# Modulation accumulations queued behind the last split of weights, and each partition sum behind a named panel's gate, in the last phase of a two-layer backbone

## The chip, the cores and the metric

The kernel runs on one core of a Trainium2 chip. A core has TensorE (PE in the profile; its weight loads are the row PEld), VectorE (DVE), ScalarE (ACT), GpSimd (POOL) and SyncE (SP), each with its own queue that it works through in order, and 16 DMA engines. The metric is the device time of one execution in microseconds (us); the time of a kernel is the median of its runs.

## What is computed

Two layers act on 256 latent rows of 1024 columns, and the first also on 256 context rows. Each layer is feed-forward, mixer, feed-forward; the mixer is attention in layer 0 and a short gated convolution in layer 1. All data are float32.

```python
for i in range(2):
    m = (silu(c) @ ada_w[i] + ada_b[i]).reshape(9, D)     # shift, scale, gate of three sub-layers
    x = half_step_ffn(x, m[0], m[1], m[2], ...)
    hx = modulate(x, m[3], m[4])                          # x * (1 + scale) + shift
    y = attention(hx) if i == 0 else short_conv_mixer(hx)
    x = layer_norm(ALPHA * x + m[5] * y)
    x = half_step_ffn(x, m[6], m[7], m[8], ...)
# half_step_ffn: a, u = modulate(x) @ w_in; y = (silu(a) * u) @ w_out;
#                x = layer_norm(ALPHA * x + 0.5 * gate * y)
```

The nine vectors of a layer come from a product of one row with a 1024 x 9216 matrix. Here they are called the modulation, and vector m of layer l is (l, m).

## The kernel before

**Products.** Every float32 weight tile is split into a high part (ACT, line 216) and the rest, the low part (DVE, line 219), and a product is made of three matmuls: high by high, low by high, high by low (lines 170 to 173, `mmu`). A unit is 256 rows by 512 columns of a weight, 512 KB. It is loaded by SP (line 211), then split in two halves on each engine, 128x512 each. Raw tiles have 4 buffers, high parts 4 and low parts 5, and two more pairs in the last phase. The names are `w1r`, `w1h`, `w1l` for the first matrix of a feed-forward, `w2...` for the second, `wc...` and `wo...` for those of the convolution.

**Stages.** A first matrix is worked through in panels (`panels`): panel p is 512 columns, its units are used for both latent tiles t = 0 and 1, and at its end ACT and DVE make the gate, `sil` = silu(a) * u (lines 503 and 504), once for each tile. A feed-forward has eleven panels, p = 0 to 10. The second matrix is worked through by `out_gemm` in a skewed order in which tile 1 follows five units behind tile 0, so that a unit stays in use longer. At its end follow the residual and the norm (`res`, `x`, `st`, `mv` on DVE, `rs` on POOL, `x` again), the transposes `hT`, and `h`, `hTh`, `hTl`, the input of the next panels. PE's order is written out by hand; the order on the other engines is made by the framework's scheduler when the program is built.

**The last phase** holds the second feed-forward of layer 0 (panels from about 590 us, second matrix from 714), the first of layer 1 (from 778, second matrix from 900), the convolution (from 964) and the last feed-forward (from 1060).

**The modulation stream.** `ada` loads `ada_w` in slices of 128 rows by 1024 columns (`ar`, 512 KB, three buffers) and adds each, times its element of silu(c), to an accumulator `acc` on DVE (line 301 for a vector's first slice, line 303 for the others), two instructions of 128x512 for a slice. Eight slices make a vector. A step of the stream is taken at a rate for each unit of PE work; in the last phase the rate is `ADA_SLOWEST`. An accumulation may not stand ahead of the newest gate multiply on DVE (`gate_ins`). In the last phase, marked by `on_pool`, `sum_up` then makes the sum over the 128 partitions on POOL (line 349, `PARTITION_ALL_REDUCE` in the profile), adds it to the bias in DRAM (line 350) and closes with a small instruction (line 352). It is called when a feed-forward's panel p in `SUM_AT` is done, at the end of the panels (`need`), and in the convolution at the end of a panel from the second on. Five vectors are made so: (1, 4) to (1, 7) in one stream, and (1, 8) in the last feed-forward.

Of the kernel before, what the change touches and what calls it, by code (L numbers as in the profile page):

```python
# [10 lines left out]
F32 = mybir.dt.float32  # L11
# [3 lines left out]
ALU = mybir.AluOpType  # L15
# [3 lines left out]
P = 128  # L19
# [13 lines left out]
WB = (4, 5, 5)  # L33
PB = {"mm": 3, "at": 3, "tp": 2}
W_EARLY = 40
ADA_SLOW, ADA_FAST, ADA_SLOWEST = 3, 0.6, 0.115
KT_IDLE = 6
BIAS_AT = 24
ADA_LATE = 20
# [29 lines left out]
E0 = (0,)  # L69
E2 = (0, 5, 7)  # L70
HOLD = 4
SUM_AT = (2, 5, 8)


@with_exitstack
def backbone_kernel(
# [6 lines left out]
    nc = tc.nc  # L83
# [10 lines left out]

    uid = [0]
    w_early = [0]
    last_split = []
    ext = [1, 0]
    ada_late = [0]

# [84 lines left out]
    def wunit(srcs, kn, s, own=None, wd=512, put_off=False):  # L185

        raw = wp.tile([P, UN], F32, tag="wr", bufs=WB[0], name=nm(s + "r"))
        if own:  # L190
            hs, ls = ([act(F32R, s + c) for _ in range(kn)] for c in "hl")
            rv = raw[:, :kn * 512].rearrange("p (a b) -> p a b", a=kn)
            with tc.high_priority(offset=w_early[0]):
                for src, c in srcs:
                    sync.dma_start(rv[:, :, c:c + src.shape[2]], src)
                for i in range(kn):
                    with queued(own[i]):
                        nc.scalar.activation(hs[i], rv[:, i], AF.Copy)
                        nc.vector.tensor_tensor(out=ls[i], in0=rv[:, i], in1=hs[i].bitcast(F32), op=ALU.subtract)
            return Parts(hs), Parts(ls)  # L200
        ext[1] += 1
        if ext[0] and ext[1] % (5 + ext[0]) in (E0 if ext[0] == 1 else E2):
            hi = hp.tile([P, UN], F32R, tag="whx", bufs=ext[0], name=nm(s + "h"))
            lo = hp.tile([P, UN], F32R, tag="wlx", bufs=ext[0], name=nm(s + "l"))
        else:
            hi = wp.tile([P, UN], F32R, tag="wh", bufs=WB[1], name=nm(s + "h"))
            lo = wp.tile([P, UN], F32R, tag="wl", bufs=WB[2], name=nm(s + "l"))
        rv, hv, lv = (t[:, :kn * wd].rearrange("p (a b) -> p a b", a=kn) for t in (raw, hi, lo))
        with tc.high_priority(offset=w_early[0]):
            for src, c in srcs:  # L210
                sync.dma_start(rv[:, :, c:c + src.shape[2]], src)

        def parts():
            m = kn * wd
            for a in range(0, m, m // W_HI):
                last_split[:] = [nc.scalar.activation(hi[:, a:a + m // W_HI], raw[:, a:a + m // W_HI], AF.Copy)]  # L216
            for a in range(0, m, m // W_LO):
                b = a + m // W_LO
                nc.vector.tensor_tensor(out=lo[:, a:b], in0=raw[:, a:b], in1=hi[:, a:b].bitcast(F32), op=ALU.subtract)  # L219
            return hv, lv  # L220

        if put_off:
            return parts
        with tc.high_priority(offset=w_early[0]):
            return parts()
# [18 lines left out]
    lnc = cp.tile([P, 2], F32, tag="lnc", name="lnc")  # L244
# [4 lines left out]
    warm = cp.tile([1, 1], F32, tag="warm", name="warm")  # L249
# [27 lines left out]

    bias_rows = []
    on_pool = [False]
    sums = []  # L280
    gate_ins = []

    def ada(vecs):
# [3 lines left out]

        def accumulate(l, m, k, w):
            with ExitStack() as st:
                for i in gate_ins:  # L290
                    st.enter_context(tc.issue_after(i.ins))
                for i, vec in enumerate(vecs):
                    if vec[:2] != (l, m):
                        continue
                    if k == 0:
                        acc[i] = hp.tile([P, D], F32, tag="acc", bufs=2, name=nm("acc"))
                    sc = cst[:, k, vec[2]:vec[2] + 1]
                    for h in range(2):
                        src, a = (c[:, h * 512:(h + 1) * 512] for c in (w, acc[i]))
                        if k == 0:  # L300
                            nc.vector.tensor_scalar(a, src, sc, None, op0=ALU.mult)
                        else:
                            nc.vector.scalar_tensor_tensor(out=a, in0=src, scalar=sc, in1=a,  # L303
                                                           op0=ALU.mult, op1=ALU.add)
            if on_pool[0] and k == KC - 1:
                sums.extend((vec, acc[i]) for i, vec in enumerate(vecs) if vec[:2] == (l, m))
# [36 lines left out]
        yield 1  # L343

    def sum_up():
        while sums:
            (l, m, v), a = sums.pop(0)
            red = hp.tile([P, D], F32, tag="red", name=nm("red"))
            nc.gpsimd.partition_all_reduce(red, a, P, ReduceOp.add)
            nc.gpsimd.dma_start(scr[l][v:v + 1, m * D:(m + 1) * D], red[0:1], accum_op=ALU.add)  # L350
            if not sums:
                nc.gpsimd.tensor_tensor(out=warm, in0=red[0:1, 0:1], in1=lnc[0:1, 0:1], op=ALU.add)
# [47 lines left out]
    def queued(ins):  # L400

        es = ExitStack()
        for i in ins:
            es.enter_context(tc.issue_after(i.ins))
        return es
# [91 lines left out]
    def gated(func, finish, s, by_dma=0):  # L497
# [3 lines left out]
        def done(p, t, bk):  # L501
            g = sp.tile([P, 256], F32, tag="s2", bufs=S2, name=nm("sil"))
            nc.scalar.activation(g, bk[:, 0:256], func)
            gate_ins[:] = [nc.vector.tensor_tensor(out=g, in0=g, in1=bk[:, 256:512], op=ALU.mult)]
            if p < by_dma:
                if t == 0:
                    part[p] = hp.tile([P, 4, 256], U16, tag="halT", bufs=3, name=nm("halT"))
                halves = hp.tile([P, 2, 256], U16, tag="hal", bufs=2, name=nm("hal"))
                nc.scalar.activation(halves, g.bitcast(U16).rearrange("p (f s) -> p s f", s=2), AF.Copy)
                sync.dma_start_transpose(part[p][:, :, t * P:(t + 1) * P], halves.rearrange("p s f -> p (s f)"))  # L510
                if t == 1:
                    def joined():
                        w = sp.tile([P, 512], F32, tag="tmp", bufs=3, name=nm("gTw"))
                        with queued(last_split):
                            nc.scalar.activation(w.bitcast(U16).rearrange("p (f s) -> p s f", s=2),
                                                 part.pop(p).rearrange("p (s j) n -> p s (j n)", s=2), AF.Copy)
                        return finish(p, w)

                    res.append(Late(D_LAG, joined))
                return  # L520
# [245 lines left out]
    for fh, (p0, p1) in enumerate(parts):  # L766
        gT = []
        for p in range(p0, p1):
            units = u0 if p == 0 else [f0_unit(p, u) for u in range(KC // F0_KN[F0[p][1]])]
            for j in range(F0[p][1]):  # L770
                if p == 0:
                    bk = b0[j]
# [421 lines left out]
    cdone, yT = gated(AF.Copy, lambda p, ps: conv(p - 2, ps), "uT")  # L1194

    def done(p, t, bk):
        if t == 1 and p > 0:
            sum_up()
        if p >= 2:
            return cdone(p, t, bk)  # L1200
        b = sp.tile([P, 512], F32, tag="s2", bufs=S2, name=nm("bs"))
        nc.scalar.activation(b, bk, AF.Copy)
        bs[p, t] = b
        if t == 1:
            for j in range(2):
                def rest(j=j):
# [73 lines left out]
```

## Time and profile before

| | us |
|---|---|
| median of 3 runs | 1252.53 (1252.21 to 1253.8) |
| profiled execution, its own time | 1251.97 |
| its span, from first to last instruction | 1250.2 |
| PE busy | 1229.4 (98%) |
| DVE busy | 965.3 (77%) |
| ACT busy | 645.2 (52%) |
| POOL busy | 82.4 (7%) |
| granted TensorE clock, mean | 0.998 |

A row of the timeline reads: start in us from the span's start, time taken, engine, line, operation, output and inputs with the buffer numbers left out, shape, number of instructions merged, and in brackets how long the engine was idle before and what released it. Successive DVE instructions overlap by some 0.08 us, so that two halves of a split of 0.69 us each show as 1.29.

### The profile page before, as it was taken

How to read it: one execution, taken by the hardware profiler on the slowest of the kernel's cores; microseconds unless marked ns; L12 is line 12 of the kernel's file. 1: busy time of each engine (PE TensorE's matmuls, PEld its weight loads, DVE VectorE, ACT ScalarE, POOL GpSimd, SP SyncE). 2: the span in 40 equal slices, each digit the busy share in tenths (PEclk: the TensorE clock that was granted, in tenths of full speed). 3: DMA queues.
4: the chain of work that ended last, by engine and by line, in shares of the span. 5: the costliest groups of instructions: out<-in, count | busy, mean ns of one | idle time of the engine just before them, and what ended most of it. 6: DMA issues, size and time to landing. Idle time of an engine off the chain costs nothing.

```text
span 1250.2 us, 17238 instructions
## 1 busy us (share of the span) xinstructions
PE 1229.4 (98%) x5794; PEld 994.1 (80%) x5794; DVE 965.3 (77%) x1675; ACT 645.2 (52%) x1233; POOL 82.4 (7%) x85
## 2 busy tenths in 40 slices
PE   8999999999999999999999999999999999999997
PEld 5787778778778878777888878888878887888886
DVE  3598987888878867888877866877777798878646
ACT  2433132322325556587678535678635644677631
POOL 0000000000001011120000200020010020002000
PEclk9999999999999999999999999999999999999999
DMA  9877679778852654554899876899886775899941
GB/s 295 301 241 235 183 236 303 248 263 277 278 186 80 183 119 85 113 110 144 262 295 290 256 252 197 218 283 300 274 266 186 222 225 159 220 294 245 276 153 68
DMA packets 232304, 275.67 MB, mean 221 GB/s; under 512 B 59622, under 2 KB 178910, under 8 KB 232216
## 3 DMA queue, kind: packets, MB, share of 16 engines
q1 hardware_dynamic: 232020, 274.54, 73.3%
q8 instruction: 45, 0.74, 0.2%
q14 instruction: 43, 0.35, 0.1%
q0 software_dynamic: 160, 0.02, 0.1%
q10 hardware_dynamic: 36, 0.02, 0.0%
HBM read 265.27 MB, written 2.20 MB: 214 GB/s over the span
## 4 chain that ended last, share of the span: by engine, by line
PE 83%; DVE 6%; DMA 4%; ACT 3%; issue 2%; SPq 1%; POOL 0%; DVEq 0%; ACTq 0%
PE f L720 19%; PE w L171 17%; PE w L170 17%; PE w L173 16%; DMA ar<-in_ada_w_dram 3%; PE wc L170 2%; PE wc L171 2%; PE wc L173 2%; PE wkv L170 1%; PE wkv L171 1%; PE wkv L173 1%; PE hT L446 1%; DVE w2l L219 1%; ACT pr L1023 1%; PE S L1015 1%
## 5 line engine op out<-in xcount | busy, mean ns | idle before, releaser
L219 DVE TENSOR_TENSOR w1l<-w1r,w1h 128x512 fp32r<-128x512 f32 (+1 forms) x352 | 230.0, 697 | 47.7 <-ACT w1h L216 46.5
L216 ACT ACTIVATE w1h<-w1r 128x512 fp32r<-128x512 f32 (+1 forms) x352 | 198.7, 618 | 115.6 <-DMA w1r<-in_ffn_w_in_dram 64.4
L170 PE MATMUL w<-w1h,hTh 128*128 128x512 f32 x528 | 206.3, 391 | 1.2 <-ACT hTh L118 1.2
L171 PE MATMUL w<-w1l,hTh 128*128 128x512 f32 x528 | 205.7, 390 | 0.0
L303 DVE SCALAR_TENSOR_TENSOR acc<-ar,cst,acc 128x512 f32<-128x512 f32 x266 | 186.9, 745 | 15.1 <-DMA ar<-in_ada_w_dram 15.0
L171 PE MATMUL w<-w2l,gh 128*128 128x512 f32 (+1 forms) x446 | 172.8, 388 | 3.6 <-DVE w2l L219 3.6
L216 ACT ACTIVATE w2h<-w2r 128x512 fp32r<-128x512 f32 x176 | 101.6, 624 | 143.3 <-PE w L173 107.8
L170 PE MATMUL w<-w2h,gh 128*128 128x512 f32 (+1 forms) x446 | 173.5, 390 | 0.0
L219 DVE TENSOR_TENSOR w2l<-w2r,w2h 128x512 fp32r<-128x512 f32 x176 | 118.2, 710 | 59.1 <-ACT w2h L216 58.3
L173 PE MATMUL w<-w1h,hTl 128*128 128x512 f32 x528 | 162.6, 389 | 0.0
L173 PE MATMUL w<-w2h,gl 128*128 128x512 f32 (+1 forms) x446 | 136.2, 386 | 0.0
L720 PE MATMUL f<-h0h,w1h 128*128 128x512 f32 x352 | 132.8, 393 | 1.0 <-ACT w1h L216 0.6
L720 PE MATMUL f<-h0l,w1h 128*128 128x512 f32 x352 | 133.2, 391 | 0.0
L720 PE MATMUL f<-h0h,w1l 128*128 128x512 f32 x352 | 132.8, 390 | 0.0
L170 PEld LDWEIGHTS w<-w1h,hTh 128*128 128x128 f32 x528 | 99.1, 188 | 22.4 <-ACT hTh L118 2.1
L173 PEld LDWEIGHTS w<-w1h,hTl 128*128 128x128 f32 x528 | 99.1, 188 | 20.9
L171 PEld LDWEIGHTS w<-w1l,hTh 128*128 128x128 f32 x528 | 99.1, 188 | 20.6 <-DVE w1l L219 0.3
L171 PEld LDWEIGHTS w<-w2l,gh 128*128 128x128 f32 x446 | 83.8, 188 | 22.3 <-DVE w2l L219 6.0
L170 PEld LDWEIGHTS w<-w2h,gh 128*128 128x128 f32 x446 | 83.8, 188 | 19.2 <-issue 1.7
L173 PEld LDWEIGHTS w<-w2h,gl 128*128 128x128 f32 x446 | 83.3, 188 | 17.0
L720 PEld LDWEIGHTS f<-h0h,w1h 128*128 128x128 f32 x352 | 65.5, 188 | 19.5 <-issue 4.2
L720 PEld LDWEIGHTS f<-h0l,w1h 128*128 128x128 f32 x352 | 65.6, 188 | 14.3 <-issue 1.0
(193 smaller groups left out, 1765.0 us busy)
## 6 DMA issues: line engine op xcount, KB each, us to landing
w1r<-in_ffn_w_in_dram SPq DMA_DIRECT2D x340, 256.0 KB
ar<-in_ada_w_dram SPq DMA_DIRECT2D x128, 512.0 KB
w2r<-in_ffn_w_out_dram SPq DMA_DIRECT2D x88, 512.0 KB
ar<-in_ada_w_dram SPq DMA_DIRECT2D x32, 256.0 KB
wkvr<-in_na_w_qkv_dram SPq DMA_DIRECT2D x32, 256.0 KB
wcr<-in_sc_w_in_dram SPq DMA_DIRECT2D x32, 256.0 KB
wqr<-in_na_w_qkv_dram SPq DMA_DIRECT2D x8, 512.0 KB
wor<-in_na_w_out_dram SPq DMA_DIRECT2D x8, 512.0 KB
```

Of the source, the lines that this page charges most:

```text
L170: nc.tensor.matmul(ps, lh, rh, start=first and i == 0, stop=False)
L171: nc.tensor.matmul(ps, lh, rl, start=False, stop=False)
L173: nc.tensor.matmul(ps, ll, rh, start=False, stop=last and i == n - 1)
L216: last_split[:] = [nc.scalar.activation(hi[:, a:a + m // W_HI], raw[:, a:a + m // W_HI], AF.Copy)]
L219: nc.vector.tensor_tensor(out=lo[:, a:b], in0=raw[:, a:b], in1=hi[:, a:b].bitcast(F32), op=ALU.subtract)
L303: nc.vector.scalar_tensor_tensor(out=a, in0=src, scalar=sc, in1=a, op0=ALU.mult, op1=ALU.add)
L446: nc.tensor.transpose(ps[:, k * P:(k + 1) * P], z[h][:, k * P:(k + 1) * P], ident)
L720: nc.tensor.matmul(ps, w, hT0[k][part == 1], start=(k == part == 0), stop=(k == KC - 1 and part == 1))
L1015: nc.tensor.matmul(banks[i], (qh, qh, ql)[f][ps, qs], (kh, kl, kh)[f][ps, :], start=f == 0, stop=f == 2)
L1023: nc.scalar.activation(pr, S, AF.Exp, bias=mx[:, 0:1], accum_out=mx[:, 1:2])
```

## The change

Three things are done. In the last phase an accumulation may not stand ahead of the last instruction of the newest low split either (`last_lo`), and the rate goes from 0.115 to 0.13 of a step for each unit. `sum_up` first places a small POOL instruction (line 347 of the changed kernel) that reads the newest gate tile, and the partition sum is queued behind it. And it is called at panels 2, 4, 6 and 7 of a feed-forward instead of 2, 5 and 8, and in the convolution after the gate of a panel instead of ahead of it.

```diff
-ADA_SLOW, ADA_FAST, ADA_SLOWEST = 3, 0.6, 0.115
+ADA_SLOW, ADA_FAST, ADA_SLOWEST = 3, 0.6, 0.13
...
-SUM_AT = (2, 5, 8)
+SUM_AT = (2, 4, 6, 7)
...
-                nc.vector.tensor_tensor(out=lo[:, a:b], in0=raw[:, a:b], in1=hi[:, a:b].bitcast(F32), op=ALU.subtract)
+                last_lo[:] = [nc.vector.tensor_tensor(out=lo[:, a:b], in0=raw[:, a:b], in1=hi[:, a:b].bitcast(F32),
+                                                      op=ALU.subtract)]
...
-                for i in gate_ins:
+                for i in gate_ins + (last_lo if on_pool[0] else []):
                     st.enter_context(tc.issue_after(i.ins))
...
     def sum_up():
+        mark = [nc.gpsimd.tensor_tensor(out=warm, in0=g[0:1, 0:1], in1=lnc[0:1, 0:1], op=ALU.add)
+                for g in last_gate[:len(sums)]]
         while sums:
             (l, m, v), a = sums.pop(0)
             red = hp.tile([P, D], F32, tag="red", name=nm("red"))
-            nc.gpsimd.partition_all_reduce(red, a, P, ReduceOp.add)
+            with queued(mark):
+                nc.gpsimd.partition_all_reduce(red, a, P, ReduceOp.add)
...
             gate_ins[:] = [nc.vector.tensor_tensor(out=g, in0=g, in1=bk[:, 256:512], op=ALU.mult)]
+            last_gate[:] = [g]
...
     def done(p, t, bk):
-        if t == 1 and p > 0:
-            sum_up()
         if p >= 2:
-            return cdone(p, t, bk)
+            cdone(p, t, bk)
+            if t == 1:
+                sum_up()
+            return
         b = sp.tile([P, 512], F32, tag="s2", bufs=S2, name=nm("bs"))
         nc.scalar.activation(b, bk, AF.Copy)
         bs[p, t] = b
+        last_gate[:] = [b]
+        if p == t == 1:
+            sum_up()
```

The order on PE is the same in both programs. DVE's order changes where accumulations stand, SP's where their slices are loaded. Two places on DVE and one on POOL follow.

DVE before, between the last panels and the second matrix of layer 0's second feed-forward (718 to 731 us). `acc` is the accumulator of vector (1, 5), `gcol` the columns of the next modulation, `w2l_7101` to `w2l_7145` low parts of three successive units; `gl`, the low part of a gate for each latent tile, stands just ahead of these rows:

```order
L303 SCALAR_TENSOR_TENSOR acc_7014<-ar_7229,cst,acc_7014 128x512 x2
L391 COPY gcol_7067<-mcT_7065 128x32
L392 SCALAR_TENSOR_TENSOR gcol_7067<-gcol_7067 128x8
L393 SCALAR_TENSOR_TENSOR gcol_7067<-gcol_7067 128x8
L303 SCALAR_TENSOR_TENSOR acc_7014<-ar_7333,cst,acc_7014 128x512
L394 TENSOR_TENSOR gcol_7067<-gcol_7067 128x8
L303 SCALAR_TENSOR_TENSOR acc_7014<-ar_7333,cst,acc_7014 128x512
L303 SCALAR_TENSOR_TENSOR acc_7014<-ar_7428,cst,acc_7014 128x512
L219 TENSOR_TENSOR w2l_7101<-w2r_7099,w2h_7100 128x512 x2
L303 SCALAR_TENSOR_TENSOR acc_7014<-ar_7428,cst,acc_7014 128x512
L219 TENSOR_TENSOR w2l_7121<-w2r_7119,w2h_7120 128x512 x2
L219 TENSOR_TENSOR w2l_7145<-w2r_7143,w2h_7144 128x512 x2
```

The same place of the changed program; the unit that was `w2l_7101` is `w2l_7110`:

```order
L119 TENSOR_TENSOR gl_7019<-gT_7013,gh_7018 128x512
L119 TENSOR_TENSOR gl_7053<-gTw_7050,gh_7052 128x512
L395 COPY gcol_7072<-mcT_7070 128x32
L396 SCALAR_TENSOR_TENSOR gcol_7072<-gcol_7072 128x8
L397 SCALAR_TENSOR_TENSOR gcol_7072<-gcol_7072 128x8
L398 TENSOR_TENSOR gcol_7072<-gcol_7072 128x8
L219 TENSOR_TENSOR w2l_7110<-w2r_7108,w2h_7109 128x512 x2
L219 TENSOR_TENSOR w2l_7130<-w2r_7128,w2h_7129 128x512 x2
L219 TENSOR_TENSOR w2l_7150<-w2r_7148,w2h_7149 128x512 x2
L219 TENSOR_TENSOR w2l_7170<-w2r_7168,w2h_7169 128x512 x2
L304 SCALAR_TENSOR_TENSOR acc_6858<-ar_7104,cst,acc_6858 128x512 x2
L219 TENSOR_TENSOR w2l_7199<-w2r_7197,w2h_7198 128x512 x2
```

The accumulations of three slices (`ar_7229`, `ar_7333`, `ar_7428`) that stood ahead of the first unit's split, and between its neighbours, are gone from there; a slice now follows every third or fourth unit's split further on. The same is so at the second matrix of layer 1's first feed-forward.

DVE before, at the start of layer 1's panels (775 to 781 us), where `hTl` is the low part of the transposed input, `res` and `x` the residual of the other tile:

```order
L219 TENSOR_TENSOR w1l_7540<-w1r_7538,w1h_7539 128x512 x2
L219 TENSOR_TENSOR w1l_7559<-w1r_7557,w1h_7558 128x512 x2
L119 TENSOR_TENSOR hTl_7463<-h_7461,hTh_7462 128x512
L411 SCALAR_TENSOR_TENSOR res_7496<-w_1392_7312,gate_6953 128x512
L416 SCALAR_TENSOR_TENSOR x_5256<-x_5256,res_7496 128x512
```

And in the changed program:

```order
L219 TENSOR_TENSOR w1l_7549<-w1r_7547,w1h_7548 128x512 x2
L219 TENSOR_TENSOR w1l_7568<-w1r_7566,w1h_7567 128x512 x2
L304 SCALAR_TENSOR_TENSOR acc_6858<-ar_7449,cst,acc_6858 128x512 x2
L119 TENSOR_TENSOR hTl_7472<-h_7470,hTh_7471 128x512
L415 SCALAR_TENSOR_TENSOR res_7505<-w_1394_7321,gate_6959 128x512
L420 SCALAR_TENSOR_TENSOR x_5256<-x_5256,res_7505 128x512
```

One slice's accumulation now stands between the splits and `hTl`.

POOL before, the second partition sum (vector (1, 5)), behind the two norms that precede layer 1's panels:

```order
L427 TENSOR_TENSOR rs_7502<-mv_7500,lnc 128x1
L428 TENSOR_TENSOR rs_7502<-rs_7502,lnc 128x1
L349 ISA
L349 ISA red_7860<-acc_7014 128x1024
L350 DMA scr_117<-red_7860 16x1x64
```

In the changed program:

```order
L431 TENSOR_TENSOR rs_7511<-mv_7509,lnc 128x1
L432 TENSOR_TENSOR rs_7511<-rs_7511,lnc 128x1
L347 TENSOR_TENSOR warm<-sil_7864,lnc 1x1
L353 ISA
L353 ISA red_7871<-acc_6858 128x1024
L354 DMA scr_117<-red_7871 16x1x64
```

The sum now waits for `sil_7864`, tile 1's gate of panel 2. The other sums wait, in order of time, for tile 1's gate of panel 10 of layer 0's second feed-forward (sum 1), of panel 10 of layer 1's first (sum 3), for tile 1's `bs` of the convolution's panel 1 (sum 4), and for tile 1's gate of panel 7 of the last feed-forward (sum 5).

More of the change, by code (lines that the diff above doesn't have):

```diff
@@ L96, in backbone_kernel @@
     w_early = [0]
-    last_split = []
+    last_split, last_lo = [], []
     ext = [1, 0]
@@ L279, in backbone_kernel @@
     on_pool = [False]
-    sums = []
+    sums, last_gate = [], []
     gate_ins = []
```

## The prediction

> **What bounds the kernel now.** I read the page first: the busy line, and one group of ACT's (busy us, mean ns, then the idle time ahead of it and what ended it).
>
> ```profile
> PE 1229.4 (98%) x5794; PEld 994.1 (80%) x5794; DVE 965.3 (77%) x1675; ACT 645.2 (52%) x1233; POOL 82.4 (7%) x85
> L216 ACT ACTIVATE w2h<-w2r 128x512 fp32r<-128x512 f32 x176 | 101.6, 624 | 143.3 <-PE w L173 107.8
> ```
>
> PE is busy for 1229.4 of 1250.2 us and its order does not change, so the change can take away only time in which PE stands still, and can cost only by making it stand. The second line says how the second matrices run: of the 143.3 us that ACT idles ahead of its high splits, 107.8 end when PE frees a buffer, not when a load lands. So the next view is PE's waits from 600 to 1062 us (engine, what it waited for: us, times, longest), and the waits themselves in PE's timeline.
>
> ```profile
> PE w L171 <- DVE w2l L219: 3.6, 3, 1.8
> PE uT L528 <- DVE sil L504: 0.2, 1, 0.2
> ```
>
> ```profile
> 729.91 0.50 PE L171 MATMUL w<-w2l,gh 128*128 128x512 f32 x1 [1.78 <-DVE w2l L219]
> 914.69 0.50 PE L171 MATMUL w<-w2l,gh 128*128 128x512 f32 x1 [1.40 <-DVE w2l L219]
> 1056.94 1.06 PE L446 MATMUL hT<-ident,x 128*128 128x128 f32 x8 [0.59 <-DVE x L438]
> 1060.04 0.49 PE L170 MATMUL w<-w1h,hTh 128*128 128x512 f32 x1 [0.63 <-ACT hTh L118]
> ```
>
> The three waits for `w2l` are 1.78 at the first boundary between panels and second matrix, and 1.40 and 0.44 at the second one. With 0.22 for `sil` in the convolution and the two of the last rows, this is all that PE loses in these 460 us: 5.06. The most that the change can win is there.
>
> **Why the low splits are late.** Two things are on DVE's queue ahead of them: a partition sum that blocks DVE, and accumulations. POOL's and DVE's timelines show the first.
>
> ```profile
> 706.45 6.33 POOL L349 PARTITION_ALL_REDUCE red<-acc  x1 [108.35 <-DVE acc L303]
> 811.18 8.26 POOL L349 PARTITION_ALL_REDUCE red<-acc  x1 [27.78 <-DVE acc L303]
> 1140.80 6.46 POOL L349 PARTITION_ALL_REDUCE red<-acc  x1 [75.83 <-DVE acc L303]
> 1140.58 6.83 DVE L219 TENSOR_TENSOR w1l<-w1r,w1h 128x512 fp32r<-128x512 f32 x4
> 1147.93 2.49 DVE L219 TENSOR_TENSOR w1l<-w1r,w1h 128x512 fp32r<-128x512 f32 x4
> 706.12 6.22 DVE L219 TENSOR_TENSOR w2l<-w2r,w2h 128x512 fp32r<-128x512 f32 x3
> ```
>
> Four halves of a split take 2.49 us, and 6.83 when a sum starts under them: one half is held for 4.34, and then DVE runs on while POOL still shows the sum. At 706 the held half ended about 5.3 us after POOL began (706.12, two free halves and one held, to 711.7). The second sum's POOL span was 8.26, longer than the others.
>
> ```profile
> 725.40 1.41 DVE L303 SCALAR_TENSOR_TENSOR acc<-ar,cst,acc 128x512 f32<-128x512 f32 x2 [2.94 <-DMA ar<-in_ada_w_dram]
> 729.17 1.28 DVE L219 TENSOR_TENSOR w2l<-w2r,w2h 128x512 fp32r<-128x512 f32 x2
> 727.75 0.39 PE L170 MATMUL w<-w2h,gh 128*128 128x512 f32 x1
> 725.20 1.16 ACT L216 ACTIVATE w2h<-w2r 128x512 fp32r<-128x512 f32 x2 [4.76 <-PE w L173]
> 714.80 0.38 ACT L503 ACTIVATE sil<-w 128x256 f32<-128x256 f32 x1 [0.98 <-PE w L173]
> ```
>
> The second is plain here: DVE waits 2.94 us for a slice's DMA, adds it, adds two more, and only at 729.17 splits a unit whose high part ACT had from 725.20 on. PE wanted the low part 0.22 after 727.75.
>
> **First boundary, after: 1.78 goes.** ACT's `sil` ends at 715.18, DVE's multiply (0.42) at 715.66; the POOL instruction that reads it takes about half a us (a small one on POOL is 0.52 in the row of 958.82 below), so sum 1 starts at 716.4 instead of 706.45 and the half that it holds ends 5.3 later, at 721.7. Behind it, in the order shown, stand three accumulation halves (2.0, a pair being 1.33 of the queue: 1.41 less the overlap), two `gl` (of a split half's shape, 0.6 each) and `gcol` (0.4: before, five halves, 3.33, and `gcol` filled DVE from 725.40 to 729.17): DVE is free at 725.3. The first high half comes at 725.83, the low halves at 726.5 and 727.1, and PE reads at 727.97. DVE could be 1.9 us later still: 0.5 until the high half, 1.4 until PE.
>
> **Second boundary: 1.84 goes.**
>
> ```profile
> 900.38 0.42 DVE L504 TENSOR_TENSOR sil<-sil,w 128x256 f32<-128x256 f32 x1 [0.84 <-ACT sil L503]
> 910.36 1.16 ACT L216 ACTIVATE w2h<-w2r 128x512 fp32r<-128x512 f32 x2 [4.76 <-PE w L173]
> 912.90 0.39 PE L170 MATMUL w<-w2h,gh 128*128 128x512 f32 x1
> ```
>
> The gate is there at 900.80, so sum 3 starts at 901.5 (before: 903.5) and its held half ends at 906.9. Then a split half (0.6), an accumulation pair (1.3), `gl` (1.2) and `gcol` (0.4) make 910.4; the first high half is there at 910.97, the low halves at 911.7 and 912.3, and PE reads at 913.13. About 2 us are to spare.
>
> **Start of layer 1's panels: 0.7 is added.** A pair now stands ahead of `hTl`, and its place is tight.
>
> ```profile
> 797.12 1.41 DVE L303 SCALAR_TENSOR_TENSOR acc<-ar,cst,acc 128x512 f32<-128x512 f32 x2
> 778.05 0.69 DVE L119 TENSOR_TENSOR hTl<-h,hTh 128x512 fp32r<-128x512 f32 x1 [0.36 <-ACT hTh L118]
> 779.53 0.61 PE L173 MATMUL w<-w1h,hTl 128*128 128x512 f32 x2
> 778.17 0.61 PE L173 MATMUL w<-w2h,gl 128*128 128x512 f32 x2
> 778.83 0.69 DVE L411 SCALAR_TENSOR_TENSOR res<-w,gate 128x512 f32<-128x512 f32 x1
> 783.43 1.00 DVE L438 TENSOR_SCALAR x<-x,mv,rs 128x512 f32<-128x512 f32 x2 [0.72 <-POOL rs L428]
> 784.07 1.08 PE L446 MATMUL hT<-ident,x 128*128 128x128 f32 x8
> ```
>
> DVE ends its splits at 777.69 (it idles 0.36 ahead of `hTl`); the pair takes it to 778.94 at least, so `hTl` ends at 779.63 and PE, at 779.53, waits 0.1. `res` began at 778.83 because PE's last product ended at 778.78; now it begins at 779.55, and the chain behind it (`x`, `st`, `mv`, POOL's `rs`, `x`) moves by the same 0.72: `x` at 784.15, its first half at 784.70. PE would transpose at 784.07, so it loses about 0.65, in which the 0.1 is contained. Bounds: nothing, if slack in the chain takes it up, and 1.3 for a whole pair. I take 0.7, nearest to the rows.
>
> **Sum 2, behind panel 2's gate: nothing.**
>
> ```profile
> 821.50 0.42 DVE L504 TENSOR_TENSOR sil<-sil,w 128x256 f32<-128x256 f32 x1 [0.37 <-ACT sil L503]
> 828.78 0.39 PE L171 MATMUL w<-w1l,hTh 128*128 128x512 f32 x1
> 829.23 0.39 PE L171 MATMUL w<-w1l,hTh 128*128 128x512 f32 x1
> ```
>
> The gate ends at 821.92, the sum starts at 822.7, the held half ends at 828.0 and its neighbour at 828.6; PE reads them at 828.78 and 829.23. The cover is 0.6 us: a block longer by that is paid for in full.
>
> **Sum 4, behind the convolution's panel 1: 0.1 is added, 0.22 goes.**
>
> ```profile
> 988.63 0.60 ACT L1202 ACTIVATE bs<-wc 128x512 f32<-128x512 f32 x1 [0.76 <-PE wc L173]
> 993.13 1.29 DVE L822 TENSOR_TENSOR x<-x,lnb 128x512 f32<-128x512 f32 x2 [0.80 <-DMA lnb<-in_ln_b_dram]
> 1000.36 0.92 DVE L504 TENSOR_TENSOR sil<-sil,wc 128x256 f32<-128x256 f32 x2
> 1004.32 0.60 PE L528 MATMUL uT<-ident,sil 128*128 128x128 f32 x4
> ```
>
> `bs` is there at 989.23, the sum starts at 989.9 instead of 1002.74. From 989.83 to 1000.36 DVE works through one queue with a single idle time, the 0.80 for `lnb`. The block adds 4.34 less that 0.80, so the gates start at 1003.9 and end at 1004.3 and 1004.6, where PE transposes from 1004.32. That costs nothing to 0.2; I take 0.1. The wait of 0.22 at 1016 stood behind the old place.
>
> **The rest: nothing.**
>
> ```profile
> 958.82 0.52 POOL L427 TENSOR_TENSOR rs<-mv,lnc 128x1 f32<-128x1 f32 x1 [39.22 <-DVE mv L425]
> 736.27 1.29 DVE L219 TENSOR_TENSOR w2l<-w2r,w2h 128x512 fp32r<-128x512 f32 x2 [1.43 <-ACT w2h L216]
> 738.99 1.29 DVE L219 TENSOR_TENSOR w2l<-w2r,w2h 128x512 fp32r<-128x512 f32 x2 [1.43 <-ACT w2h L216]
> 741.07 0.39 PE L171 MATMUL w<-w2l,gh 128*128 128x512 f32 x1
> ```
>
> Sum 5 moves from 1140.80 to about 1152.9 and meets the same kind of stretch, whose splits bore the block without a wait of PE. What stands behind a sum on POOL is the `rs` of a norm; behind sum 3 POOL idled 39 us for it, so the waits that are added there hold nobody up. The rate only moves slices; their number stays. In the second matrices a pair now follows a unit's split: DVE idles 1.43 us ahead of a unit and a pair takes 1.33, so it fits if its slice is there.
>
> **The sum.** −1.78 −1.84 −0.22 +0.7 +0.1 = −3.04. The profiled execution took 1251.97, so 1248.9; the median of the runs is 0.56 above it, so 1249.5.
>
> [...] The row: at 706 the held half ended a us before POOL's sum did. [...]
>
> **The rivals.**
>
> *Each block lasts to the end of POOL's span, or as long as sum 2's.* The held half then ends 7.1 to 7.2 after the start, 1.8 later. The boundaries bear it (1.9 and 2 to spare), sum 2 costs 1.8 − 0.6 = 1.2, sum 4 a further 1.8: 1252.5, no change. For it: the span of 8.26, under the same kind of panel. Against: at 706 and at 1140 alike one half was held for 4.34.
>
> *The second boundary isn't cured.* Sum 3 only moves by 2 us and still stands in the boundary; if a slice is late there as at 725.40 (2.94), the 2 us to spare are gone and 0.9 to 1.8 stay: 1250.4 to 1251.3, no change. Against: only one pair is left there.
>
> *Late slices in the second matrices: slower.* DVE's queue is in order, so a pair whose slice has not landed holds the next unit's split, in a stretch where units come just in time. By the late slice at 725.40 a pair costs 2.94 + 1.33 − 1.43 − 1.24 = 1.6, where 1.24 is what a unit's second low half (740.28) has to spare ahead of PE (0.45 behind 741.07). It begins to cost from a slice that is 1.34 late. Each of the two second matrices has about four pairs; if half of the eight are late, 6.4 are added: 1255.9. Against: by SP's order a slice is issued three units or more (2.72 us each, 736.27 to 738.99) before its pair.
>
> *DVE is relieved further.* Without sum 4's block at 1002.74 and a slice less behind it, the residuals before 1056.94 may come earlier, and 0.59 and 0.63 go too: 1248.3.
>
> **How the numbers follow.** A measurement of this kernel tells 0.2%, 2.5 us, from no change: faster is below 1250.0, slower above 1255.0. The forecast has 0.52; with the bounds of its added terms (0 to 1.3 and 0 to 0.2) its own range is 1248.7 to 1250.2, of which 0.03 lies above 1250.0. The relieved DVE has 0.08, the longer block 0.16, the uncured boundary 0.10. Late slices have 0.14: two late pairs (1252.7) 0.04, four 0.10. So faster is 0.57, the same 0.33, slower 0.10. The range goes from 1247.8 (0.5 under the best case) to 1253.0, above the longer block and two late pairs.
>
> **What would show it.** PE's waits for `w2l` near 730 and 915 gone; a wait for `x` of 0.5 to 0.8 near 784 and none for `w1l` near 828; `uT` near 1004 with 0.2 at most; five sums at 716, 823, 902, 990 and 1153, each with one DVE half held for 4.3. Wrong would be: held halves of 6 us or more; accumulations in 730 to 770 and 915 to 950 that wait for DMA, with waits for `w2l` behind them; or waits at the boundaries as before.

## The result and the profile after

| | before | after |
|---|---|---|
| median, first comparison (6 runs each) | 1252.24 us | 1247.83 us (1245.57 to 1248.64) |
| ratio, first comparison | | 0.9963 (0.9951 to 0.9976) |
| ratio of a second comparison (5 runs against 15 of before) | | 0.9957 (0.9944 to 0.9969) |
| profiled execution, own time | 1251.97 us | 1247.93 us |
| its span | 1250.2 us | 1246.1 us |
| PE busy | 1229.4 us | 1227.6 us |

The change makes the kernel faster by 4.4 us in the first comparison and by 5.7 in the second (the medians of its befores and its runs, 1253.02 and 1247.35). The forecast was 3.0 faster, with a range that began at 1247.8: the direction is right, but the gain is about half as large again, and the time lies at the range's lower edge (by the first ratio, 0.9963 × 1252.24 = 1247.6, just outside). So the question is where more came from than the sum had.

PE's waits in the profile after, from 600 to 1062 us (the two of the list that the change was to act on):

```profile
PE w L171 <- DVE w2l L219: 1.1, 1, 1.1
PE uT L533 <- DVE sil L508: 0.6, 1, 0.6
```

The wait near 730 is gone; one near 912 is left, and `uT` waits longer than before. POOL's timeline says why (the small instruction that reads the gate, and the sum behind it, for sums 1, 3 and 4):

```profile
714.63 0.63 POOL L347 TENSOR_TENSOR warm<-sil,lnc 1x1 f32<-1x1 f32 x1 [117.60 <-DVE sil L508]
720.86 6.13 POOL L353 PARTITION_ALL_REDUCE red<-acc  x1 [5.60 <-issue]
...
898.32 0.56 POOL L347 TENSOR_TENSOR warm<-sil,lnc 1x1 f32<-1x1 f32 x1 [59.12 <-DVE sil L508]
906.59 6.13 POOL L353 PARTITION_ALL_REDUCE red<-acc  x1 [7.71 <-issue]
...
985.42 0.18 POOL L347 TENSOR_TENSOR warm<-bs,lnc 1x1 f32<-1x1 f32 x1 [20.12 <-ACT bs L1208]
992.56 6.29 POOL L353 PARTITION_ALL_REDUCE red<-acc  x1 [6.96 <-issue]
```

The forecast had each sum half a us behind its small instruction. It starts 5.6 to 7.7 us behind the end of it, in idle time for which the profile shows no reason. DVE's timeline shows what it then holds:

```profile
722.75 2.67 DVE L396 SCALAR_TENSOR_TENSOR gcol<-gcol 128x8 f32<-128x8 f32 x1
...
906.65 4.49 DVE L398 TENSOR_TENSOR gcol<-gcol 128x8 f32<-128x8 f32 x1
911.07 2.49 DVE L219 TENSOR_TENSOR w2l<-w2r,w2h 128x512 fp32r<-128x512 f32 x4
...
992.17 8.63 DVE L219 TENSOR_TENSOR wcl<-wcr,wch 128x512 fp32r<-128x512 f32 x7
```

Sum 1 falls on a `gcol` of 0.16 and into DVE's own spare time. Sum 3 falls on the last `gcol` ahead of the unit's split, which so begins at 911.07 and is late. Sum 4 falls on splits ahead of the convolution's gates.

**Where the time went, stretch by stretch.** PE's order is the same in both programs, so the start of each PE instruction in one trace can be set against its start in another. The table gives by how much a stretch (in before's clock) took longer than in the first trace of before. "Lead" is the offset that a trace has at 600 us already, where no instruction was moved.

| trace | lead | 720 to 735 | 775 to 800 | 905 to 930 | 990 to 1010 | 1010 to 1040 | 600 to 1242 |
|---|---|---|---|---|---|---|---|
| before, second | 0.04 | +2.31 | -0.01 | -0.40 | 0.00 | -0.01 | +1.87 |
| before, third | -1.95 | +2.00 | -0.02 | +0.29 | 0.00 | -0.01 | +2.24 |
| before, fourth | -1.33 | +0.33 | +0.03 | -0.03 | 0.00 | -0.01 | +0.29 |
| after, first | -1.08 | -2.22 | +0.68 | -1.25 | +0.91 | -0.55 | -2.46 |
| after, second (again) | -1.22 | -2.22 | +0.68 | -1.89 | 0.00 | -0.55 | -3.98 |
| after, third | -1.42 | -2.22 | +0.67 | -1.67 | +0.76 | -0.56 | -3.09 |
| touch | 0.44 | -2.19 | +0.68 | -2.83 | +0.53 | -0.57 | -4.40 |
| touch_rate_0125 | -0.95 | -2.20 | +0.67 | -2.83 | -0.01 | -0.55 | -4.19 |
| touch_rate_0135 | -0.61 | -2.19 | +0.10 | -2.83 | +0.76 | -0.55 | -4.74 |
| touch_rate_0115 | -0.04 | -2.22 | +0.68 | -2.79 | +0.43 | +3.48 | +0.87 |
| gates_only | -1.32 | +0.71 | -0.01 | -0.59 | +1.11 | +1.87 | +3.06 |
| no_sum | -1.23 | -2.19 | +0.67 | -2.83 | 0.00 | -0.55 | -5.11 |

(touch_rate_0125 and touch_rate_0115 lose a further 0.67 and 1.36 between 930 and 990.) Three things stand out. The 1.78 of idle time at the first boundary was worth 2.22, and the 1.84 at the second 2.83. Before itself varies by 2.3 at the first boundary; after does not at all. And the lead is scatter: before shows 0.04 to -1.95 there, with the same instructions.

### The profile page after: what moved, and what is told of

Read it like the earlier page. It is cut to its first block, busy times and chain, and to the rows that moved or that the text cites. A ratio compares the mean times of both kernels' runs of the same rounds, so it can differ in the third digit from the quotient of the medians.

```text
span 1246.1 us, 17225 instructions
## 1 busy us (share of the span) xinstructions
PE 1227.6 (99%) x5794; PEld 994.6 (80%) x5794; DVE 964.0 (77%) x1675; ACT 644.7 (52%) x1233; POOL 81.7 (7%) x90
## 4 chain that ended last, share of the span: by engine, by line
PE 87%; DVE 4%; DMA 4%; ACT 2%; issue 2%; SPq 1%; POOL 0%; DVEq 0%; ACTq 0%
PE f L725 19%; PE w L170 17%; PE w L171 17%; PE w L173 17%; PE wkv L170 2%; PE wkv L171 2%; PE wkv L173 2%; DMA ar<-in_ada_w_dram 2%; PE wc L170 1%; PE wc L173 1%; PE wc L171 1%; DMA wor<-in_na_w_out_dram 1%; PE S L1020 1%; PE hT L450 1%; DMA wcr<-in_sc_w_in_dram 1%
## 5 line engine op out<-in xcount | busy, mean ns | idle before, releaser
L219 DVE TENSOR_TENSOR w2l<-w2r,w2h 128x512 fp32r<-128x512 f32 x176 | 113.9, 687 | 54.7 <-ACT w2h L216 53.3
```

The source lines that it names most:

```text
L219: last_lo[:] = [nc.vector.tensor_tensor(out=lo[:, a:b], in0=raw[:, a:b], in1=hi[:, a:b].bitcast(F32), op=ALU.subtract)]
```

## The experiments

**The changed kernel again (again).** No edit.

> The changed kernel once more, nothing edited. In the first pair of traces PE's offset between the two programs is -1.08 us before 590 us, where their instructions are the same, -2.46 from there to 1242 us, and -0.5 behind PE's last product. Theory: only the middle part belongs to the change, so here the middle part is again within 0.2 of -2.46 against the trace of before, the first and last parts come out otherwise (by 0.5 us or more), and the median gain over five rounds is nearer to 2.5 than to 4.4. Rival: all three parts belong to the change; then the first part is again within 0.3 of -1.08, and the median gain stays at 4 us or more.

Measured: lead -1.22, middle part -3.98, ratio 0.9957. The theory fell on all three readings, as it was put. What it took for the change's fixed effect varies by 1.5 between two executions of one program, at the second boundary and at 1004, the two places of the late sums. The rival's two figures came out, but not for its reason: the third and fourth traces of before have such a lead too, with nothing changed.

**The queue alone (queue_only).**

```
-                for i in gate_ins:
+                for i in gate_ins + (last_lo if on_pool[0] else []):
...
-ADA_SLOW, ADA_FAST, ADA_SLOWEST = 3, 0.6, 0.115
+ADA_SLOW, ADA_FAST, ADA_SLOWEST = 3, 0.6, 0.13
```

> The accumulations queued behind the last low split and the rate of 0.13; no gates, sums called where the kernel before calls them. Theory (the queue wins at the two boundaries, the gates only keep the sums out of harm's way): the waits for w2l at 730 and 915 are gone (3.6 us), but by POOL's order sum 2 now stands between the norms of the two latent tiles at 770 to 782 us, so tile 1's rs waits for the sum (6.3), its DMA (1) and the closing preparation (7): PE waits about 11 us near 784, and perhaps as much again near 955, where sum 4 stands ahead of a norm; 1258 to 1275 us. Rival (the gates carry the gain): the waits for w2l stay at 3 us or more and the time is 1252 or above without a new wait for x.

Measured: 1275.41 us, ratio 1.0181 (1.0165 to 1.0196), just above what was expected. The waits for `w2l` are gone, and two long ones for `x` have come. POOL's timeline (`rs` of tile 0 ahead, the sum, its DMA, `rs` of tile 1) and PE's:

```profile
777.65 6.61 POOL L350 PARTITION_ALL_REDUCE red<-acc  x1 [6.69 <-DVE res L412]
784.56 1.00 POOL L351 DMA_DIRECT2D scr<-red  x1 [0.31 <-POOL red L350]
794.38 0.18 POOL L428 TENSOR_TENSOR rs<-mv,lnc 128x1 f32<-128x1 f32 x1 [8.82 <-issue]
```

```profile
795.89 1.97 PE L447 MATMUL hT<-ident,x 128*128 128x128 f32 x8 [14.63 <-DVE x L439]
```

The sum costs POOL 6.6, its DMA 1, and then 8.8 go by ahead of the next ordinary instruction. The next PE instructions are late by 16.5 us here, and near 961 (in before's clock) by some 13 more. More than the idle time is lost because TensorE still runs at half clock behind the wait: its rows start 0.43 apart until 799.4 and 0.23 apart from 799.84 on. The mean granted clock of this trace is 0.988, where the first trace of before has 0.998. So the queue brings the gain at the boundaries (the stretch from 720 to 735 is 2.19 shorter here, that from 905 to 930 2.79), and cannot stand alone: with the faster rate and no gate, a sum comes between the norms of the two tiles. Whether the queue or the rate puts it there was not tested.

**The gates alone (gates_only).** The changed kernel with `for i in gate_ins:` and a rate of 0.115.

> The gates, the new panels and the convolution's new place for the sums, with the rate of 0.115 and accumulations not queued behind low splits. Theory (the queue wins at the boundaries): the wait for w2l near 730 stays at 1.5 us or more, since the three slices still stand ahead of that unit; at the second boundary sum 3 comes later (in the convolution), so only part of 1.8 stays; gain 0 to 2 us. Rival (the gates carry the gain): both waits go and the gain is 3 us or more.

Measured: 0.9996 (0.9986 to 1.0006) over 11 runs. PE's waits, the two that matter:

```profile
PE w L171 <- DVE w2l L219: 3.8, 2, 2.5
PE uT L533 <- DVE sil L508: 2.9, 2, 2.1
```

Both waits for `w2l` stay, and two sums in the convolution add 2.9. The gain of the change is not the gates'.

**The gate through DVE (touch).**

```
-        mark = [nc.gpsimd.tensor_tensor(out=warm, in0=g[0:1, 0:1], in1=lnc[0:1, 0:1], op=ALU.add)
-                for g in last_gate[:len(sums)]]
+        mark = []
+        for (_, s), g in zip(sums, last_gate):
+            nc.vector.scalar_tensor_tensor(out=s[:, 0:1], in0=g[:, 0:1], scalar=0.0, in1=s[:, 0:1],
+                                           op0=ALU.mult, op1=ALU.add)
...
-            with queued(mark):
-                nc.gpsimd.partition_all_reduce(red, a, P, ReduceOp.add)
+            nc.gpsimd.partition_all_reduce(red, a, P, ReduceOp.add)
```

> The changed kernel with POOL's small instruction taken away; in its place DVE, behind the same gate, adds zero times a column of the gate to a column of the accumulator, so that the sum waits for the gate through DVE. Theory (the sums of the changed kernel start 6 to 8 us behind their gates because POOL's preparation for the sum stands behind the small instruction): the preparation now runs early, the sums start within 1.5 us of their gates (about 715, 818, 899 and 986), as the forecast had it; the wait of 1.13 for w2l near 912 and that of 0.6 for uT near 1001 go; PE's offset to before, from 590 to 1242 us, is -3.0 to -4.2 instead of -2.46. Rival (the 6 to 8 us are something of the sum itself or of its own wait): the sums start 6 to 8 us behind the gates as before, and the waits stay.

Measured: 1246.55 us, 0.9952 (0.9939 to 0.9964). POOL's sums 1, 3 and 4, and what sum 1 holds on DVE:

```profile
717.02 6.34 POOL L354 PARTITION_ALL_REDUCE red<-acc  x1 [118.48 <-DVE acc L349]
...
900.64 6.44 POOL L354 PARTITION_ALL_REDUCE red<-acc  x1 [64.06 <-issue]
...
988.34 6.46 POOL L354 PARTITION_ALL_REDUCE red<-acc  x1 [23.10 <-DVE acc L349]
```

```profile
716.68 5.62 DVE L219 TENSOR_TENSOR w2l<-w2r,w2h 128x512 fp32r<-128x512 f32 x2
```

The sums now start 0.14 to 0.25 us behind the end of DVE's small addition. So the delay of 6 to 8 us belongs to the step from an ordinary POOL instruction to a sum. We take it for preparation, the `ISA` row without a tile that stands ahead of each sum in POOL's order; the profile has no row that shows it at work, so this was not shown. Before, and here, it follows the last ordinary instruction, and POOL is idle for long ahead of the sum (23.10 to 118.48 us in the rows above). In the changed kernel it stands behind the small instruction, which is an ordinary one. The second boundary is clean (-2.83), and the held half took 5.62 for two halves that take 1.28: 4.34, as forecast. The wait at 1001 did not go altogether (0.53 stays): the small addition for sum 4 stands in DVE's queue, so that this sum still starts 3.1 us behind its gate and not within 1.5 as expected. The last phase won 4.40, a little over what was expected, as waits are dearer than their idle time (below).

**Before again (before_again).** No edit.

> The kernel before once more, nothing edited. The trace of the changed kernel is 1.1 us ahead of before's at 590 us, where nothing was moved; its second trace and two other kernels show 1.0 to 1.4 there as well. Theory: the first trace of before was a slow one in that part (loads at the start, the first 35 us), so this one lies 0.5 to 1.5 ahead of it at 590; the ratio is 1. Rival: the early 1.1 us is the change's own; then this trace agrees with the first of before within 0.3 at 590. From 590 on both say an offset that does not move by more than 0.3.

Measured: ratio 0.9998 (0.9986 to 1.001), lead 0.04 (so the theory on the lead fell), and from 600 us on not the same within 0.3 but 1.87 longer, nearly all of it at the first boundary. PE's timeline there:

```profile
730.62 0.50 PE L171 MATMUL w<-w2l,gh 128*128 128x512 f32 x1 [2.48 <-DVE w2l L219]
...
732.06 0.63 PE L170 MATMUL w<-w2h,gh 128*128 128x512 f32 x1
732.49 0.63 PE L171 MATMUL w<-w2l,gh 128*128 128x512 f32 x1
```

Matmuls that lie 0.23 apart elsewhere lie 0.43 apart here. The table of stretches (us, PE busy, granted clock, DMA share, GB/s) says what that is, this trace first and the first trace of before below:

```profile
732.00:735.50 3.50, 3.50 (x10) 0.51 0.84 274
```

```profile
732.00:735.50 3.50, 3.50 (x17) 1.00 0.79 223
```

The slice landed 0.7 later than in the first trace (DVE takes it at 726.11 and not at 725.40), PE waited 2.48, and the clock was halved for 3.4 us behind the wait.

**No sums (no_sum).** POOL doubles one row of the accumulator in place of each sum over partitions, which is left out.

> The changed kernel without the sum over partitions: POOL doubles one row of each accumulator instead, which leaves out five sums and their blocks of DVE. Theory (a wait of PE costs its idle time as the timeline gives it plus 0.4, since matmul rows overlap by 0.16 and the first one behind a wait takes 0.5 and not 0.23): against the first trace of the changed kernel, PE gains 1.5 at the second boundary, where the timeline shows 1.13 of idle time, and 0.8 at the convolution's first uT, where it shows 0.60; the boundary at 730 and the 0.65 at 780 to 784 stay as they are. Rival (idle time is what a wait costs): 1.1 and 0.6.

Measured: 1246.06 us, 0.9950 (0.9933 to 0.9968). Against the first trace of the changed kernel PE gains 1.58 at the second boundary and 0.91 at the first `uT`. A wait costs more than its idle time, here by 0.3 to 0.45; the rival's 1.1 and 0.6 don't hold. POOL's rows bear on the delay as well:

```profile
714.44 0.62 POOL L347 TENSOR_TENSOR warm<-sil,lnc 1x1 f32<-1x1 f32 x1 [117.56 <-DVE sil L508]
715.02 2.34 POOL L353 TENSOR_TENSOR red<-acc 1x1024 f32<-1x1024 f32 x1
```

Behind the same small instruction, an ordinary instruction starts at once (715.02): the 6 to 8 us stand ahead of the sum and not ahead of this one. This is also the most that better places for the sums can bring: 5.11 against 2.46 to 3.98 in the last phase.

**Other rates (touch_rate_0125, touch_rate_0135, touch_rate_0115).** The kernel of the run touch with one number changed.

> The kernel of the run touch with a rate of 0.125 in place of 0.13, by which no accumulation stands between the splits and hTl at 778 us; a pair stands at other units instead. Theory (that pair costs 0.65: the 0.25 at hTl and the 0.42 at hT): PE's two steps at 779.8 and 784 are gone, the rest is as in touch, so PE's offset to before from 590 to 1242 us goes from -4.4 to -5.0. Rival (the steps there come from elsewhere, such as the late slices): they stay at 0.5 or more.

> The kernel of the run touch with a rate of 0.135, by which no accumulation stands ahead of hTl at 778; the first slice of a vector, whose two instructions are shorter (0.8 of the queue), stands ahead of hTl at 788 instead. Theory: the steps of 0.25 and 0.42 at 780 and 784 are gone and 0 to 0.3 comes at 788, so PE's offset to before from 590 to 1242 us is -4.7 to -5.1, the best so far. Rival: the steps move to 788 in full, as with the rate of 0.125 (+0.64), and the offset stays at -4.4.

> The kernel of the run touch with the old rate of 0.115: accumulations queued behind the last low split, sums behind their gates, and slices at the old pace. Theory (the queue alone clears the boundaries, the rate only shifts slices so that four sums find their vectors in time): the step of -2.2 at 730 is there, and -2.75 at 915 to 920 too, since the slices stand behind the unit's split; sum 4 falls later in the convolution and costs there 0.5 to 2.5 us. Rival (the gain hangs on the rate): a wait for w2l of 1 us or more is back at 730 or 915.

With 0.125 (0.9955) the two steps at 780 and 784 went and came back 5 us later, at the next `hTl`, which now has the pair ahead of it; with 965, where a further pair does the same, nothing is won:

```profile
786.03 0.74 PE L173 MATMUL w<-w1h,hTl 128*128 128x512 f32 x2 [0.36 <-DVE hTl L119]
```

With 0.135 they went (0.10 is left), and the ratio is 0.9950 (0.9934 to 0.9965), the best trace of all but no_sum; the runs do not part it from the changed kernel. With 0.115 both boundaries are clean too (-2.22 and -2.79), so the queue does that at either rate; gates_only, at the same rate without the queue, has +0.71 and -0.59 there (the two also differ in the kind of gate). But it is no faster than before (0.9992): vectors come later, two sums fall into the convolution, and one of the waits that they cause, 2.12 us long, is followed by half clock (0.50 from 1028.0 to 1031.4, 1.00 in the stretches on either side; +3.48, where 0.5 to 2.5 was expected).

```profile
1026.70 0.44 PE L534 MATMUL uT<-ident,sil 128*128 128x128 f32 x2 [2.12 <-DVE sil L509]
```

**A wait of known place (stall_short, stall_mid, stall_long).** The kernel of the run touch with 14, 20 or 27 small additions behind `gcol`, and the low splits queued behind them.

```
+                for _ in range(14):
+                    with queued([e]):
+                        hold[:] = [nc.vector.tensor_tensor(out=d[:, 0:P], in0=ident, in1=ident, op=ALU.add)]
...
+                with queued(hold):
                     last_lo[:] = [nc.vector.tensor_tensor(out=lo[:, a:b], ...
```

> The kernel of the run touch, with 14 small DVE additions (128x128, about 0.2 us of the queue each) behind gcol at the first boundary, and the next unit's low split queued behind them, so that PE waits for w2l there by about 1.1 us of idle time. [...] Rival (a wait costs its idle time alone): the step equals the idle time within 0.15.

> As the run stall_short, with 20 small additions: an idle time of about 2.3 us, near that of the kernel before. [...] Against touch 2.7 to 4.3 us slower. Rival: one step of idle + 0.4 alone, a spread of 2 us, and 2.7 slower.

> As the run stall_short, with 27 small additions: an idle time of about 3.7 us ahead of w2l at the first boundary. [...] Rival (the half clock of one trace of before came from something else than the wait): clock 1.0, step 4.1.

The waits came out far longer than meant (an addition takes 0.32 of the queue, 4.53 us for the 14, and an earlier unit is held too), so behind all three the clock was halved, and the short case was not had. What they give is the price of a long wait: idle time, the 0.16 by which matmul rows overlap, and half of the time at half clock that is left when PE goes on (from the trace's record of the clock; PE's rows start 0.43 apart until then). stall_short: PE's row behind the wait, and the stretches around it:

```profile
730.00 0.79 PE L171 MATMUL w<-w2l,gh 128*128 128x512 f32 x1 [3.99 <-DVE w2l L220]
```

```profile
725.90:730.00 4.10, 0.11 (x1) 0.80 0.01 3
730.00:735.00 5.00, 5.00 (x12) 0.50 0.48 165
```

| run | idle | half clock behind it | half of that | idle + 0.16 + that half | PE's step against touch |
|---|---|---|---|---|---|
| stall_short | 3.99 | 730.00 to 735.16 | 2.58 | 6.73 | 6.65 |
| stall_mid | 5.95 | 730.69 to 734.92 | 2.12 | 8.23 | 8.23 |
| stall_long | 8.24 | 731.48 to 735.03 | 1.78 | 10.18 | 10.11 |

In stall_long the rival (clock 1.0) is out, and of stall_short's question, what a short wait costs, nothing is learned; there the clock was halved for 6.8 us, 1.64 ahead of 730.00 (0.80 over 4.10 us) and 5.16 behind it. Of the spread, nothing can be said: stall_mid's 12 runs lie within 3.6 us (1253.26 to 1256.9), but all of them list a clock of 0.995 or 0.996, so there is none without the half clock to set them against.

**How often before meets the half clock (before_third, before_fourth, after_third).** No edits.

> The kernel before, a third trace. Theory (the kernel before loses 2.2 us at the first boundary at least, and 2.9 to 4.6 where the slice lands later and the clock is halved behind the wait): an idle time of 1.8 to 2.5 ahead of w2l near 730, with or without 3.4 us of clock 0.5 behind it; at 915 a loss of 2.7 as in the other two. Rival (the first trace shows the usual run): 1.78 within 0.1 and clock 1.0.

> The kernel before, a fourth trace, with the same two readings as for the third: the theory wants at least one of the two with an idle time over 2.2 or a half clock; the rival wants both like the first.

> The changed kernel, a third trace. Theory: the first boundary is without a wait in every trace; the second sum in the way (near 906) and that of the convolution (near 992) start 6.5 to 8.5 us behind their gates, and cost 0.5 to 1.6 and 0 to 0.8; no half clock anywhere between 590 and 1240 us. Rival: a wait for w2l near 730 comes back in some runs, or the clock is halved in this kernel too.

Measured: idle times of 2.31, with the half clock, and of 2.06, without. So of four traces of before two have the half clock, and the first one, on which the forecast was made, has the shortest wait of the four. The changed kernel has no wait at 730 and no half clock in any of three (in the first, 1.00 in every stretch from 590 to 1240).

The granted clock that is listed for every run says the same of many more. The four traces of before have 0.998 without the half clock, and 0.997 and 0.996 with it. Of the 56 runs of before beside which the other kernels were measured, 28 list 0.997 or less, with a mean of 1253.9 us, and 28 list 0.998 or more, with 1252.1. All 12 runs of the changed kernel list 0.998 or more. So, as an estimate from these lists, about half of before's executions meet a half clock, and it costs them 1.8 us. The figure of a run does not say where in it the clock was low; only the traces do.

## Why the prediction was off

**The step that failed first** is in the part on what bounds the kernel. It says that the change "can take away only time in which PE stands still", and of the six waits: "this is all that PE loses in these 460 us: 5.06. The most that the change can win is there." The idle time in brackets is not what a wait costs, and one execution does not show what the kernel loses. In the second trace of before PE is busy all through the 3.5 us from 732.0, and yet works on 10 matmuls there where the first trace has 17: at half clock time is lost while PE is busy. And without the sums (no_sum) the three places that were to win, with 3.84 of idle time, gave 2.19, 2.83 and 0.55, together 5.57, more than the 5.06 that were to be the most. The rows of PE's timeline behind those of 727.75 and 729.91, in the trace that the forecast had, show the first part:

```profile
730.25 0.39 PE L170 MATMUL w<-w2h,gh 128*128 128x512 f32 x1
730.51 0.50 PE L171 MATMUL w<-w2l,gh 128*128 128x512 f32 x1
730.85 0.62 PE L173 MATMUL w<-w2h,gl 128*128 128x512 f32 x2
```

Rows of 0.39 start 0.23 apart, so a row overlaps the next by 0.16: PE was due at 727.98 and came at 729.91, 1.93 later. Behind the wait the starts lie 0.34, 0.26 and 0.34 apart and not 0.23, another 0.26. Together 2.2, which is the table's 2.22. The waits without a half clock cost 0.3 to 0.5 more than their brackets say (0.44 here, 0.45 and 0.31 by no_sum, 0.33 at `uT` near 1016).

Term by term, against the first trace of before:

- **First boundary, 1.78.** The mechanism held: no wait is left in any of three traces. That sum 1 would be out of the way at 721.7 did not hold: it started 5.6 late, as sum 3 did, and its block did no harm because it fell on `gcol` and on 2.37 us in which DVE was idle ahead of it. The size was 2.22, and against the mean of four traces of before 2.22 + (0 + 2.31 + 2.00 + 0.33)/4 = 3.38, since a later slice and the half clock come on top in other executions. This is the largest error, 1.6 us: 0.44 is the price of a wait, and 1.16 comes from taking one profiled execution for all of them.
- **Second boundary, 1.84.** Two errors against each other. It held 2.83 (two waits, each 0.4 dearer, and some more), but only 1.25 to 1.89 of it went. What failed was "the POOL instruction that reads it takes about half a us", from which the sum was to start at once. touch shows that the place was right and the start was wrong. The number stood in the profile of before, at the end of each sum, ahead of the next ordinary instruction:

```profile
722.00 0.50 POOL L352 TENSOR_TENSOR warm<-red,lnc 1x1 f32<-1x1 f32 x1 [7.78 <-issue]
```

- **Layer 1's panels, 0.7.** Measured 0.67 to 0.68, and 0.10 where the pair is away. Right in mechanism and size.
- **Sum 2, nothing.** The number is right, but by luck as far as the changed kernel goes: the sum started 6.6 late and so held another split than the one reckoned with. In touch, where it starts 0.9 behind its gate as forecast, it costs nothing either.
- **Sum 4, 0.1 and -0.22.** The old wait was worth 0.55; the new place costs 0 to 0.91. In the first and third traces a split is held ahead of the convolution's gates; in the second POOL's row is longer (9.14 from 992.29) and DVE is held only from 996.7 on, behind both gates.
- **The sum.** -3.04 against -2.46, -3.98 and -3.09 from one trace to the other. So against the trace that it was made from the sum was about right, and that was luck: what the dearer waits added, the late sums took away. Mean against mean (three of after, four of before) it is -3.18 - 1.10 = -4.3, which comes near the gain of the medians in the first comparison, 4.4; with so few traces, and a lead that scatters by 2, it does not explain the 5.7 of the second. That more was won than forecast comes from the other executions of before, which the forecast left out.

**The rivals.** The block to the end of POOL's span did not happen: 4.34 in touch, where DVE goes on at 722.3 and POOL's row ends at 723.36. The span of 8.26, which the prediction has for this rival, is answered by DVE's row under it in before:

```profile
815.50 4.70 DVE L219 TENSOR_TENSOR w1l<-w1r,w1h 128x512 fp32r<-128x512 f32 x4 [2.05 <-ACT w1h L216]
```

Three halves ran freely from 811.56 on, behind the start of POOL's row, and these four took 2.2 more than their 2.49: a longer row held DVE later, not longer. DVE goes on 1.05 to 1.6 us ahead of the end of POOL's row (722.30 against 723.36 in touch, 911.14 against 912.72 at sum 3 of the changed kernel); why the row is longer than the hold, no run here shows. The second boundary was indeed not cured in full, but by a late sum, not a late slice. Late slices in the second matrices cost nothing: no wait for `w2l` stands there in any trace. And the waits of 0.59 and 0.63 near 1057 are in every trace, so nothing was relieved there.

## What to carry to other kernels

Price a wait by the starts of the rows around it and not by its idle time, and ask whether the clock is halved behind it, as it was here behind waits of 2.12 to 2.48 us, though not behind all; then look at a second profile, because a wait that hangs on a DMA can differ from one execution to the next (1.78, 2.48, 2.31 and 2.06 in four traces of before). Where an instruction is queued behind a marker, ask what the engine has to do between the two: a marker of another kind put 6 to 8 us between gate and sum, and the same gate taken through the data that the sum reads put 1 us or less, except where that step had to wait in DVE's queue (3.1). An accumulation that can wait belongs behind the work that PE waits for, but pulling it away moves whatever hangs on its end, here sums that came to stand between two norms, with the faster rate, and cost PE some 30 us until they were gated.

## What was not expected of the hardware

Some waits of 1.8 to 2.5 us were followed by TensorE's half clock and some were not, and their length does not part them:

| trace | wait, us | granted clock behind it |
|---|---|---|
| before, second | 2.48 | 0.51 from 732.0 to 735.5 |
| before, third | 2.31 | 0.50 from 728.8 to 732.2, then 1.00 |
| touch_rate_0115 | 2.12 | 0.50 from 1028.0 to 1031.4, then 1.00 |
| gates_only, near 729 | 2.49 | 1.00 from 727.7 to 740 |
| gates_only, near 1029 | 2.07 | no half clock: PE's rows 0.23 apart again from 1030.0 on |
| before, fourth | 2.06 | no half clock: PE's rows 0.23 apart again from 730.2 on |
| before, first | 1.78 | 1.00 from 727.7 to 740 |

Behind these three waits the half clock took 3.4 us each time; at the longer wait of stall_short (3.99) it took 6.8. The wait of 2.49 in gates_only went without it and that of 2.12 in touch_rate_0115 did not; what decides it was not shown.

In two traces of the changed kernel (the first and the third), 5.60 to 7.71 us pass between the small POOL instruction and the sum behind it. Between a sum's DMA and the next ordinary instruction it is 6.86 to 11.15 (before's first trace and touch_rate_0115), with no row in the profile for either. Where POOL had no small instruction between its long idle time and the sum, the first does not show: the sums of before at 706, 903 and 1002 start 0.14 to 0.25 us behind the end of the last accumulation, and those of touch as soon behind DVE's small addition.
